# A gap in a modulation schedule, three pinned readers and later row transposes in a macaron layer

## The chip, the cores and the metric

The kernel runs on one core of one Trainium2 chip. The metric is the device time of one execution in microseconds (us); before the change the median of three runs is 1946.7 us (1944.29 to 1949.12). Everything below about times of the kernel before comes from one more, profiled execution.

## The reference, cut to what matters

One decoder layer for 256 tokens of width 2048, all in float32. A vector `c` gives nine modulation vectors of 2048 values each; three blocks (FFN, mixer, FFN) use a shift, a scale and a gate each.

```python
mod = silu(c) @ ada_w + ada_b                      # 9 * 2048 values
sh1, sc1, gt1, sh2, sc2, gt2, sh3, sc3, gt3 = split(mod, 9)
h = rmsnorm(x, g0) * (1 + sc1) + sh1
x = x + 0.5 * gt1 * (silu(h @ wg0) * (h @ wu0)) @ wd0      # FFN 1, inner width 5632
h = rmsnorm(x, g1) * (1 + sc2) + sh2
q_f, k_f, v_f, f_f, qkv_g, a_g, b_g, z_g = split(h @ w_in)
o_f = rmsnorm(forgetting_attention(q_f, k_f, v_f, log_sigmoid(f_f + bias)))   # 8 heads of 128
q_g, k_g, v_g = split(silu(causal_conv4(qkv_g)))
o_g = gated_delta_rule(l2norm(q_g), l2norm(k_g), v_g, decay(a_g), sigmoid(b_g))  # chunks of 64
o_g = rmsnorm(o_g) * silu(z_g)                             # 8 heads of 128
x = x + gt2 * (concat(o_f, o_g) @ w_out)
h = rmsnorm(x, g2) * (1 + sc3) + sh3
x = x + 0.5 * gt3 * (silu(h @ wg1) * (h @ wu1)) @ wd1      # FFN 2
return rmsnorm(x)
```

## The kernel before, in words

**Weight blocks.** All weight matrices are packed into one list of 128x128 tiles in the order of use, eight tiles (512 KB) to a block, 674 blocks. For every block SP issues a DMA into `wraw` (line 125), ACT casts it to the rounded form `whi` (line 128), and DVE subtracts to get the rest, `wlo` (line 140); PE multiplies with both, which gives float32 accuracy. There are four buffers each of `wraw`, `whi` and `wlo`; in the two FFNs every fifth block uses a further buffer for `wraw`. The stages by block number: FFN 1 gate and up for the first 28 of 44 column groups 0 to 112, its down product 112 to 168, gate and up for the rest 168 to 232, down 232 to 264; mixer projections 264 to 378, output projection 378 to 410; FFN 2 410 to 674.

**Modulation columns.** The modulation is computed beside this stream, 128 values at a time: one *column* is a DMA of 1 MB into `adat` (line 261) and one DVE reduction of it against silu(c) (line 265). There are 144 columns in the order of first need. `RATE` is a list of (block, columns per block); at every block the rate is added to `owed` (line 143), and whenever that reaches one, the next column is asked for. A column that is needed and hasn't been asked for is asked for at once (`ada_need`, line 274). The DMA is kept behind the DMA of the newest weight block; the reduction is recorded when the stream is two blocks further (`settle`, `BEHIND = 2`), behind the split of that block.

**Order of work.** A scheduler orders the recorded instructions of each engine by their estimated times; `issue_after(X)` keeps an instruction behind X in that order. In the mixer, small pieces of work (generators) are woven into the projections: each `yield g` lets g us of estimated matmul time (0.35 us per tile of three matmuls) pass before the generator goes on. There are four queues of them: `k`, `gdn`, `fox` and `out`. Queue `k` holds in order `gates` (line 829), then `decays(0)`, `keys(0)` to `keys(3)`, `solve(0)`, and `decays(1)`, `keys(4)` to `keys(7)`, `solve(1)`.

**Small DRAM round trips.** Three kinds of data go through DRAM to be spread over the partitions. `gates` transposes the gate projections (`pcol`, line 844), computes log decays, makes rows and columns of their cumulated sums (`prow`, `pcum`, lines 877 to 886) and stores the rows; `row_of` (line 903) and `fetch_rows` (line 927) read them back into `rw` and `rowk` by SP. Readers of these are `decay(h)`, which adds a mask to `rw` into `dec` (line 914) and takes exponentials on ACT (lines 916, 917); `decays(half)`, which subtracts `rowk` from a mask into `Ln` for four heads (line 935) and takes eight exponentials (line 938); and `fox(h)`, whose mask `fm` starts as two ACT operations on `rw` (line 1184), followed by logits, a maximum (line 1195), exponentials (line 1199), and a transpose `ppt` of them on PE (line 1204). `solve` stores blocks of `Ln` (eight DMAs, line 999), reads them back, solves 16x16 systems on DVE (lines 1012, 1013), stores (line 1018) and reads the result `U` (line 1022), from which two DVE operations make `U0` (line 1025). `keys(h)` transposes a key (`pk`, line 971), makes its Gram matrix (`pkk`, line 974), takes norms (line 977) and a copy (line 978) on ACT and multiplies the Gram matrix into `Ln` (line 984).

Of the kernel before, what the change touches and what calls it, by code (L numbers as in the profile page):

```python
# [12 lines left out]
AF = mybir.ActivationFunctionType  # L13
ALU = mybir.AluOpType
PSUM = bass.MemoryType.PSUM

P = 128
# [15 lines left out]
GR = 24  # L33
NEG = -1e30

RATE = ((0, 0.5), (28, 0.25), (33, 0.5), (49, 0.25), (56, 0.5), (66, 0.2), (112, 0.5), (168, 0.42), (232, 0.24), (264, 0.0), (288, 0.285), (376, 0.0), (424, 0.16))
N_BIG, N_GDN = 3, 3
N_FIRST = 2
AHEAD = 4
# [54 lines left out]
class Stream:  # L94
# [36 lines left out]
    def next(self, mat, k, n, width=1):  # L131
        i = len(self.order)
        if i % WB == 0:
            nc = self.nc
            b = i // WB
            r, lo = self.first.pop(0) if self.first else self.block(b)
            self.l = lo.tile([P, WB * P], F32R, name="wlo")
            pace = [r_ for r_ in RATE if r_[0] <= b][-1][1]
            with self.behind():
                lo_ = nc.vector.tensor_tensor(self.l, r, self.h.bitcast(F32), ALU.subtract)  # L140
            with self.tc.issue_after(lo_.ins):
                self.settle(b - BEHIND)
            self.owed += 0.0 if self.quiet else pace
            while self.owed >= 1.0:
                self.owed -= 1.0
                self.side()
        for d in range(width):
            self.order.append((mat, k, n, width, d))
        o = (i % WB) * P
        h, l = self.h[:, o : o + width * P], self.l[:, o : o + width * P]  # L150
        return (h, l) if width == 1 else (woven(h), woven(l))
# [3 lines left out]
def layer_kernel(ctx: ExitStack, tc: tile.TileContext, xrow, c, adaw, cols, cst, w, out, order, dbg=None):  # L155
    nc = tc.nc
    V, A, G, PE = nc.vector, nc.scalar, nc.gpsimd, nc.tensor
# [26 lines left out]
    W = Stream(nc, w, raw, hi, lo)  # L184
# [40 lines left out]
    def C(name, lo_=0, n=None):  # L225
        o, wd = CST[name]
        return cstt[:, o + lo_ : o + (wd if n is None else lo_ + n)]
# [449 lines left out]
    for kind, i in (("x", 0), ("x", 1), ("c", 0), ("c", 1), ("x", 2), ("x", 3), ("c", 2), ("c", 3)):  # L677
        with nullcontext() if hold is None else tc.issue_after(hold):
            if kind == "c":
                hold = cond(i)  # L680
            else:
                t, q = divmod(i, 2)
# [70 lines left out]
    def mixer():  # L753
# [65 lines left out]
        colS = gp.tile([P, 2, 5, NH], F32, name="colS")  # L819
# [7 lines left out]
        Ln = gp.tile([P, NH, 2, P], F32, name="Ln")  # L827
        U0 = gp.tile([P, NH, 2, 64], F32, name="U0")

        def gates(ps):  # L830

            yr = x[:, 8]
            d = pt("ey")
            s = norm1.scaled(d, ps)
            A.activation(yr[R], d[R], AF.Identity, bias=s[R])
            y, ny, e, em, t0, q = (x[:, j, : 2 * GR].rearrange("p (t r) -> p t r", t=2) for j in range(10, KD))
            coef = tiny.tile([P, GR + PAD["hid"]], F32, name="coef", bufs=1)[:, :GR]
            tc.keep_in_program_order(A.activation(coef, L("alog"), AF.Exp))
            V.tensor_scalar(coef, coef, -1.0, None, ALU.mult)
            yield 2.0  # L840
            pc = psf("pcol")
            pcv = pc[:, : 2 * GR].rearrange("p (t r) -> p t r", t=2)
            for t in range(2):
                PE.transpose(pcv[:, t], yr[R, t * P : (t + 1) * P], ident[R, :GR])
            both = lambda c_: c_.unsqueeze(1).to_broadcast([P, 2, GR])
            V.tensor_tensor(y, pcv, both(L("gbias")), ALU.add)
            V.tensor_tensor(y, y, both(C("sgn")), ALU.mult)
            V.scalar_tensor_tensor(ny, y, -1.0, y, ALU.mult, ALU.min)
            A.activation(e, ny, AF.Exp)
            V.tensor_scalar(em, y, 0.0, None, ALU.min)  # L850
            A.activation(em, em, AF.Exp)

            S = ny
            V.tensor_scalar(t0, e, 2.0, None, ALU.add)
            V.reciprocal(t0, t0)
            V.tensor_tensor(S, e, t0, ALU.mult)
            V.tensor_tensor(t0, S, S, ALU.mult)
            V.tensor_scalar(q, t0, 1.0 / 17.0, None, ALU.mult)
            for n in (15, 13, 11, 9, 7, 5, 3):
                V.scalar_tensor_tensor(q, q, 1.0 / n, t0, ALU.add, ALU.mult)  # L860
            V.scalar_tensor_tensor(q, q, 1.0, S, ALU.add, ALU.mult)
            V.tensor_scalar(y, y, 0.0, None, ALU.max)
            V.scalar_tensor_tensor(y, q, 2.0, y, ALU.mult, ALU.add)
            V.tensor_tensor(y, y, both(coef), ALU.mult)

            V.tensor_scalar(t0, e, 1.0, None, ALU.add)
            V.reciprocal(t0, t0)
            V.tensor_tensor(colS[:, :, 4], em[:, :, 16:24], t0[:, :, 16:24], ALU.mult)
            yield 8.0

            fox_, gdn_ = slice(0, NH), slice(NH, 2 * NH)
            pr = psf("prow")
            po = psf("pcum")
            pcs = po[:, : 6 * NH].rearrange("p (t q r) -> p t q r", t=2, q=3)
            for t in range(2):
                sl = slice(t * P, (t + 1) * P)
                PE.matmul(pr[:NH, T + t * P : T + (t + 1) * P], y[:, t, gdn_], C("tri64"), start=True, stop=True)
                PE.matmul(pr[:NH, sl], y[:, t, fox_], C("tri"), start=True, stop=(t == 0))
                if t:
                    PE.matmul(pr[:NH, sl], y[:, 0, fox_], L("ones"), start=False, stop=True)  # L880
            for t in range(2):
                PE.matmul(pcs[:, t, 1], C("tri64"), y[:, t, gdn_], start=True, stop=True)
                PE.matmul(pcs[:, t, 2], C("tru64"), y[:, t, gdn_], start=True, stop=True)
                PE.matmul(pcs[:, t, 0], C("tri"), y[:, t, fox_], start=True, stop=(t == 0))
                if t:
                    PE.matmul(pcs[:, t, 0], L("ones"), y[:, 0, fox_], start=False, stop=True)
            rt = x[:, 8:10].rearrange("p a t -> p (a t)")[:NH]
            A.copy(rt, pr[:NH])
            nc.sync.dma_start(rows, rt)
            V.tensor_copy(colS[:, :, 0:2], pcs[:, :, 0:2])  # L890
            A.activation(colS[:, :, 2:4], pcs[:, :, 1:3], AF.Exp)
            V.tensor_tensor(nbeg, colS[:, :, 4], colS[:, :, 2], ALU.mult)
            V.tensor_scalar(nbt, colS[:, :, 4], -1.0, None, ALU.mult)
            V.tensor_scalar(ng, colS[:, :, 1], -1.0, None, ALU.mult)
            yield 2.0
            fetch_rows(0)
            yield 1.0
# [8 lines left out]
        bc = lambda c_: c_.unsqueeze(1).to_broadcast([P, 2, P])  # L906
        bh = lambda c_, n: c_.unsqueeze(1).to_broadcast([n, 2, 64])

        def decay(h):

            gb = rowg.pop(h)
            gbv = gb.rearrange("p (t j) -> p t j", t=2)
            dd = m2p.tile([P, 2, P], F32, name="dec")
            V.tensor_tensor(dd, bc(C("mU")), gbv, ALU.add)
            for t in range(2):
                A.activation(dd[:, t], dd[:, t], AF.Exp, bias=ng[:, t, h : h + 1])
            A.activation(gb, gb, AF.Exp)
            return dd, gb
# [10 lines left out]
        def decays(half):  # L929

            hs4 = slice(4 * half, 4 * half + 4)
            yield 5.0
            rv = rowk[half].rearrange("p h (t j) -> p (h t) j", t=2)
            mL = C("mL").unsqueeze(1).to_broadcast([P, 8, P])
            V.tensor_tensor(Ln[:, hs4].rearrange("p h t j -> p (h t) j"), mL, rv, ALU.subtract)
            for h in range(4 * half, 4 * half + 4):
                for t in range(2):
                    A.activation(Ln[:, h, t], Ln[:, h, t], AF.Exp, bias=colS[:, t, 1, h : h + 1])
            yield 3.0
# [46 lines left out]
        def solve(half):  # L986


            hs4, n = slice(4 * half, 4 * half + 4), 2 * NH // 2
# [14 lines left out]
            blk, xt_, pr = (x[B, j] for j in range(4, 7))  # L1004
# [15 lines left out]
            U = x[:, 7, :P].rearrange("p (n i) -> p n i", n=n)  # L1020
# [1 line left out]
                nc.sync.dma_start(U, lt[ht].rearrange("n b (q i) -> (b q) n i", q=16))  # L1022
            yield 5.0
            for q in range(2):
                V.tensor_tensor(
                    U0[:, hs4].rearrange("p h t (b i) -> p (h t) b i", b=4)[:, 4 * q : 4 * q + 4],
                    U[:, 4 * q : 4 * q + 4].unsqueeze(2).to_broadcast([P, 4, 4, 16]),
                    C("blk").unsqueeze(1).unsqueeze(3).to_broadcast([P, 4, 4, 16]), ALU.mult)
            if half == 0:
                fetch_rows(1)  # L1030
            yield 1.0
# [148 lines left out]
        def fox(h, qk, vt):  # L1180
            cb = rowf.pop(h)
            fm = m1p.tile([P, 384], F32, name="fm")
            for t, o, wd in ((0, 0, P), (1, P, T)):
                A.activation(fm[:, o : o + wd], cb[:, :wd], AF.Identity, bias=colS[:, t, 0, h : h + 1], scale=-1.0)
            V.tensor_tensor(fm, fm, C("foxm"), ALU.add)
            yield 1.5
            pl = psf("plog")
# [293 lines left out]
```

## Time and profile before

| | |
|---|---|
| median of three runs | 1946.7 us |
| the profiled execution | 1951.09 us |
| its span, first to last instruction | 1949.1 us |
| mean granted TensorE clock | 0.992 |
| blocks 0 to 112 of FFN 1 on PE | about 19 to 341 us |
| blocks 112 to 168, 168 to 232, 232 to 264 | to 494, 665, 749.5 us |
| mixer projections from block 264 | from 749.5 us |

The profiled execution took 1951.09 us, 4.4 us more than the median, and 2 us of it lie outside of the span. Lines of the profile name the engine, the source line, what is written from what, the shape, the count, the busy time and the mean of one instruction, then the idle time ahead of it and what ended most of that. The views of waits give, for a stretch of time, who waited for whom: us in total, how many times, the longest. The views of windows give, for a stretch, the busy time of PE, of its weight loads (PEld), of DVE, ACT and POOL, then the granted clock of PE, the share of the time that the 16 DMA engines were busy, and the GB/s moved.

### The profile page before, as it was taken

What the parts mean: (1) busy time and instruction counts of PE and PEld (TensorE: products, weight loads), DVE (VectorE), ACT (ScalarE), POOL (GpSimd) and SP (SyncE); (2) the same over time, 40 slices, a digit from 0 to 9 for tenths busy, and PEclk for the clock granted to TensorE, in tenths of its full rate; (3) what the DMA queues carried; (4) which work ended last, traced back from release to release, by engine and by line L of the source; (5) the groups of instructions that cost most, each with busy time, mean ns of one, the idle gap of its engine ahead of it and who ended that gap; (6) DMA issues with size and microseconds to landing.
All of it is one profiled execution on the core that took longest, in us unless ns stands there. A gap on an engine that the chain in (4) does not pass through costs nothing.

```text
span 1949.1 us, 33807 instructions
## 1 busy us (share of the span) xinstructions
PE 1906.4 (98%) x13086; PEld 1777.7 (91%) x13087; DVE 1569.0 (81%) x2455; ACT 1051.7 (54%) x1670; POOL 52.3 (3%) x55
## 2 busy tenths in 40 slices
PE   9999999999999999999999999999999999999998
PEld 7999999888889999889989999999999999999997
DVE  6999978999999999779988978887777756566654
ACT  7444544433454557848666756665554345555553
POOL 0000000000000021000000002100000000000011
PEclk9999999999999999999999999999999999999999
DMA  9988877999999886486667647677787666666663
GB/s 383 347 347 330 319 249 268 388 378 385 362 358 368 333 280 226 170 295 235 236 239 274 218 138 252 206 269 263 267 267 264 224 199 203 202 200 202 201 202 119
DMA packets 129490, 519.58 MB, mean 267 GB/s; under 512 B 18217, under 2 KB 21545, under 8 KB 111153
## 3 DMA queue, kind: packets, MB, share of 16 engines
q1 hardware_dynamic: 129330, 517.42, 74.5%
q8 instruction: 103, 1.69, 0.3%
q14 instruction: 57, 0.47, 0.1%
HBM read 512.89 MB, written 4.47 MB: 265 GB/s over the span
## 4 chain that ended last, share of the span: by engine, by line
PE 73%; DVE 13%; issue 5%; DMA 5%; ACT 2%; SPq 0%; DVEq 0%; ACTq 0%
PE pd L488 14%; PE pu L484 10%; PE pg L484 10%; PE pd L489 7%; PE pu L485 5%; PE pg L485 5%; DVE wlo L140 5%; PE po L488 3%; DVE adat L265 3%; DMA adat<-in_ada_dram 3%; PE pgu L570 2%; PE pgu L568 2%; PE pgu L569 2%; PE pp L799 2%; PE pp L797 2%
## 5 line engine op out<-in xcount | busy, mean ns | idle before, releaser
L140 DVE TENSOR_TENSOR wlo<-wraw,whi 128x1024 fp32r<-128x1024 f32 x674 | 819.6, 1222 | 255.8 <-ACT whi L128 253.4
L128 ACT CAST whi<-wraw 128x1024 fp32r<-128x1024 f32 x674 | 698.2, 1045 | 501.2 <-PE pd L488 152.7
L488 PE MATMUL pd<-hid,whi 128*128 128x512 f32 x1408 | 461.8, 382 | 0.0
L489 PE MATMUL pd<-hid,wlo 128*128 128x256 f32 x1408 | 384.5, 273 | 4.3 <-DVE wlo L140 4.3
L265 DVE CUSTOM_DVE_ANT_0 adat<-adat,cs,colt 128x2048 f32<-128x2048 f32 x142 | 333.0, 2345 | 18.1 <-DMA adat<-in_ada_dram 18.1
L484 PE MATMUL pg<-hs,whi 128*128 128x512 f32 x912 | 302.5, 382 | 0.5 <-DVE shc L432 0.5
L484 PE MATMUL pu<-hs,whi 128*128 128x512 f32 x912 | 302.3, 382 | 0.0
L488 PEld LDWEIGHTS pd<-hid,whi 128*128 128x128 f32 x1408 | 266.0, 189 | 36.6
L489 PEld LDWEIGHTS pd<-hid,wlo 128*128 128x128 f32 x1408 | 270.3, 192 | 7.2 <-DVE wlo L140 7.0
L570 PE MATMUL pgu<-hs,wlo 128*128 128x256 f32 x896 | 240.8, 279 | 13.6 <-DVE wlo L140 13.1
L485 PE MATMUL pu<-hs,wlo 128*128 128x256 f32 x912 | 249.3, 273 | 0.4 <-DVE wlo L140 0.2
L485 PE MATMUL pg<-hs,wlo 128*128 128x256 f32 x912 | 249.5, 274 | 0.0
L568 PE MATMUL pgu<-hs,whi 128*128 128x256 f32 x896 | 244.7, 276 | 0.4 <-ACT whi L128 0.3
L569 PE MATMUL pgu<-hs,whi 128*128 128x256 f32 x896 | 244.2, 276 | 0.0
L484 PEld LDWEIGHTS pg<-hs,whi 128*128 128x128 f32 x912 | 172.4, 189 | 24.7 <-ACT shc L431 0.7
L484 PEld LDWEIGHTS pu<-hs,whi 128*128 128x128 f32 x912 | 172.4, 189 | 23.6
L570 PEld LDWEIGHTS pgu<-hs,wlo 128*128 128x128 f32 x896 | 168.6, 193 | 17.5 <-DVE wlo L140 17.4
L485 PEld LDWEIGHTS pu<-hs,wlo 128*128 128x128 f32 x912 | 175.0, 192 | 2.5 <-DVE wlo L140 2.4
L485 PEld LDWEIGHTS pg<-hs,wlo 128*128 128x128 f32 x912 | 175.0, 192 | 1.1
L568 PEld LDWEIGHTS pgu<-hs,whi 128*128 128x128 f32 x896 | 172.6, 193 | 1.1 <-ACT whi L128 0.5
L797 PE MATMUL pp<-hs,whi 128*128 128x256 f32 x592 | 172.5, 291 | 0.4 <-ACT whi L128 0.4
L569 PEld LDWEIGHTS pgu<-hs,whi 128*128 128x128 f32 x896 | 172.6, 193 | 0.3 <-DVE hs L382 0.3
(346 smaller groups left out, 2653.7 us busy)
## 6 DMA issues: line engine op xcount, KB each, us to landing
wraw<-in_w_dram SPq DMA_DIRECT2D x674, 512.0 KB, 4.5
adat<-in_ada_dram SPq DMA_DIRECT2D x142, 1024.0 KB, 7.4
xr<-in_xr_dram SPq DMA_DIRECT2D x4, 512.0 KB, 5.4
adaf<-in_ada_dram SPq DMA_DIRECT2D x4, 512.0 KB, 8.6
xd<-x SPq DMA_DIRECT2D x4, 512.0 KB, 6.7
rw<-rowd SPq DMA_DIRECT2D x16, 128.0 KB, 6.2
x<-xd SPq DMA_DIRECT2D x4, 512.0 KB, 7.1
out_dram<-o SPq DMA_DIRECT2D x8, 256.0 KB, 2.8
```

Of the source, the lines that this page charges most:

```text
L128: self.cast = self.nc.scalar.copy(self.h, r).ins
L140: lo_ = nc.vector.tensor_tensor(self.l, r, self.h.bitcast(F32), ALU.subtract)
L265: V.tensor_tensor_reduce(t, t, cs, 1.0, L("adab", q, 1), ALU.mult, ALU.add, mod[:, q : q + 1])
L484: PE.matmul(ps, wt[0], both, start=(k == 0), stop=False)
L485: PE.matmul(ps[:, T:], wt[1], part(k, HI), start=False, stop=(k == KD - 1))
L488: PE.matmul(ps, wt[0], act.rearrange("p q (a b) -> p q b a", a=2), start=first, stop=False)
L489: PE.matmul(ps[:, :T], wt[1], woven(act[:, 0]), start=False, stop=last)
L568: PE.matmul(o, wh, part(k, HI), start=first and s == 0, stop=False, skip_group_check=skip)
L569: PE.matmul(o, wh, part(k, LO), start=False, stop=False, skip_group_check=skip)
L570: PE.matmul(o, wl, part(k, HI), start=False, stop=last, skip_group_check=skip)
L797: PE.matmul(pp[i][:, :T], wh, hh, start=(k == 0), stop=False)
L799: PE.matmul(pp[i][:, :T], wl, hh, start=False, stop=(k == KD - 1))
```

## The change

Four edits, none of which changes what is computed. (1) `RATE` gets an entry of zero from block 90, so that no column is asked for in blocks 90 to 111; the later rates go from 0.42 to 0.45 (168 to 231), 0.24 to 0.26 (232 to 263) and 0.285 to 0.295 (from 288), and the last of these ends at block 384 and not 376. (2) `gates` waits 4 us of estimated time and not 2 before its transposes `pcol`. (3) `decays(1)` starts after 10 us and not 5. (4) The readers of the small DRAM transfers are kept behind a split or a cast: the first operations of `decay` and `decays` and the `U0` operations of `solve` behind the newest split (`W.split`, which `Stream.next` now keeps), the two `fm` operations of `fox` behind the newest cast.

```diff
@@ -33,7 +33,7 @@
 GR = 24
 NEG = -1e30
 
-RATE = ((0, 0.5), (28, 0.25), (33, 0.5), (49, 0.25), (56, 0.5), (66, 0.2), (112, 0.5), (168, 0.42), (232, 0.24), (264, 0.0), (288, 0.285), (376, 0.0), (424, 0.16))
+RATE = ((0, 0.5), (28, 0.25), (33, 0.5), (49, 0.25), (56, 0.5), (66, 0.2), (90, 0.0), (112, 0.5), (168, 0.45), (232, 0.26), (264, 0.0), (288, 0.295), (384, 0.0), (424, 0.16))
 N_BIG, N_GDN = 3, 3
 N_FIRST = 2
 AHEAD = 4
@@ -140,6 +140,7 @@
                 lo_ = nc.vector.tensor_tensor(self.l, r, self.h.bitcast(F32), ALU.subtract)
             with self.tc.issue_after(lo_.ins):
                 self.settle(b - BEHIND)
+            self.split = lo_.ins
             self.owed += 0.0 if self.quiet else pace
             while self.owed >= 1.0:
                 self.owed -= 1.0
@@ -837,7 +838,7 @@
             coef = tiny.tile([P, GR + PAD["hid"]], F32, name="coef", bufs=1)[:, :GR]
             tc.keep_in_program_order(A.activation(coef, L("alog"), AF.Exp))
             V.tensor_scalar(coef, coef, -1.0, None, ALU.mult)
-            yield 2.0
+            yield 4.0
             pc = psf("pcol")
             pcv = pc[:, : 2 * GR].rearrange("p (t r) -> p t r", t=2)
             for t in range(2):
@@ -911,7 +912,8 @@
             gb = rowg.pop(h)
             gbv = gb.rearrange("p (t j) -> p t j", t=2)
             dd = m2p.tile([P, 2, P], F32, name="dec")
-            V.tensor_tensor(dd, bc(C("mU")), gbv, ALU.add)
+            with tc.issue_after(W.split):
+                V.tensor_tensor(dd, bc(C("mU")), gbv, ALU.add)
             for t in range(2):
                 A.activation(dd[:, t], dd[:, t], AF.Exp, bias=ng[:, t, h : h + 1])
             A.activation(gb, gb, AF.Exp)
@@ -929,10 +931,11 @@
         def decays(half):
 
             hs4 = slice(4 * half, 4 * half + 4)
-            yield 5.0
+            yield 10.0 if half else 5.0
             rv = rowk[half].rearrange("p h (t j) -> p (h t) j", t=2)
             mL = C("mL").unsqueeze(1).to_broadcast([P, 8, P])
-            V.tensor_tensor(Ln[:, hs4].rearrange("p h t j -> p (h t) j"), mL, rv, ALU.subtract)
+            with tc.issue_after(W.split):
+                V.tensor_tensor(Ln[:, hs4].rearrange("p h t j -> p (h t) j"), mL, rv, ALU.subtract)
             for h in range(4 * half, 4 * half + 4):
                 for t in range(2):
                     A.activation(Ln[:, h, t], Ln[:, h, t], AF.Exp, bias=colS[:, t, 1, h : h + 1])
@@ -1022,10 +1025,11 @@
                 nc.sync.dma_start(U, lt[ht].rearrange("n b (q i) -> (b q) n i", q=16))
             yield 5.0
             for q in range(2):
-                V.tensor_tensor(
-                    U0[:, hs4].rearrange("p h t (b i) -> p (h t) b i", b=4)[:, 4 * q : 4 * q + 4],
-                    U[:, 4 * q : 4 * q + 4].unsqueeze(2).to_broadcast([P, 4, 4, 16]),
-                    C("blk").unsqueeze(1).unsqueeze(3).to_broadcast([P, 4, 4, 16]), ALU.mult)
+                with tc.issue_after(W.split):
+                    V.tensor_tensor(
+                        U0[:, hs4].rearrange("p h t (b i) -> p (h t) b i", b=4)[:, 4 * q : 4 * q + 4],
+                        U[:, 4 * q : 4 * q + 4].unsqueeze(2).to_broadcast([P, 4, 4, 16]),
+                        C("blk").unsqueeze(1).unsqueeze(3).to_broadcast([P, 4, 4, 16]), ALU.mult)
             if half == 0:
                 fetch_rows(1)
             yield 1.0
@@ -1181,7 +1185,8 @@
             cb = rowf.pop(h)
             fm = m1p.tile([P, 384], F32, name="fm")
             for t, o, wd in ((0, 0, P), (1, P, T)):
-                A.activation(fm[:, o : o + wd], cb[:, :wd], AF.Identity, bias=colS[:, t, 0, h : h + 1], scale=-1.0)
+                with tc.issue_after(W.cast):
+                    A.activation(fm[:, o : o + wd], cb[:, :wd], AF.Identity, bias=colS[:, t, 0, h : h + 1], scale=-1.0)
             V.tensor_tensor(fm, fm, C("foxm"), ALU.add)
             yield 1.5
             pl = psf("plog")
```

From here on each reduction and split is counted by its block. In the order of the changed kernel columns 36 to 41 are asked for behind the DMAs of blocks 112, 114, 116, 118, 120 and 122, where it was 90, 95, 100, 105, 110 and 113 (counted from 0; each later column of FFN 1 comes 6 to 10 blocks later than before, columns 100 and 101 come at 289 and 292 instead of 252 and 256, the rest 7 to 4 later in the mixer and 2 earlier in FFN 2). Column 127, which was forced by its use at block 410, is now asked for by rate at 380. By stretches, 6 columns were asked for in blocks 90 to 113 and now one; in 114 to 167 it is 27 in both; in 168 to 231 it is 27 before and 29 now, in 232 to 263 it is 6 and 7, and in 288 to 383 it is 25 and 28. All lines from 143 on have moved by one to five.

On DVE, behind the split of block 87, before (line 265 is a reduction, lines 586, 587, 519 and 503 are the ends of gate and up products):

```order
L140 TENSOR_TENSOR wlo<-wraw,whi 128x1024
L265 ISA adat,mod<-adat,cs,colt 128x2048
L265 ISA mod 128x1
L586 TENSOR_TENSOR tg<-pgu,acc 128x256
L587 TENSOR_TENSOR tu<-pgu,acc 128x256
L140 TENSOR_TENSOR wlo<-wraw,whi 128x1024
L519 TENSOR_TENSOR tu<-tu,tg 128x256
L140 TENSOR_TENSOR wlo<-wraw,whi 128x1024
L503 TENSOR_TENSOR hid<-tu,hid 128x256
```

and in the changed kernel, from the splits of blocks 87 and 88:

```order
L140 TENSOR_TENSOR wlo<-wraw,whi 128x1024 x2
L587 TENSOR_TENSOR tg<-pgu,acc 128x256
L588 TENSOR_TENSOR tu<-pgu,acc 128x256
L520 TENSOR_TENSOR tu<-tu,tg 128x256
L140 TENSOR_TENSOR wlo<-wraw,whi 128x1024
L504 TENSOR_TENSOR hid<-tu,hid 128x256
```

The reduction between two splits is gone; the same holds behind the splits of blocks 92, 97, 102, 107 and 111. The first reduction of the changed kernel after that of column 35 stands behind the split of block 109, four element operations later.

On ACT in the mixer, from the casts of blocks 283 and 284 on, before (`j` and `kk` are of `keys(0)`, `fm` of `fox(0)`, `kbd` of the first `gdn`, `Ln` of `decays(0)`; ACT_TABLE_LOAD loads another function table):

```order
L128 CAST whi<-wraw 128x1024 x2
L977 ACTIVATE j_9118,ssk<-pk 128x128
L977 ACTIVATE j_9120,ssk<-pk 128x128
L978 COPY kk<-pk 128x256
L1184 ACTIVATE fm<-rw,colS 128x128
L1184 ACTIVATE fm<-rw,colS 128x256
L1084 ACTIVATE kbd<-kk,colS 128x128
L938 ACT_TABLE_LOAD
L938 ACTIVATE Ln<-Ln,colS 128x128 x8
L959 ACT_TABLE_LOAD
```

and in the changed kernel, from the cast of block 283 on, with the cast of block 284 in the fifth row:

```order
L128 CAST whi<-wraw 128x1024
L962 ACT_TABLE_LOAD
L962 ACTIVATE kk<-cv 128x256
L959 ACTIVATE cv<-cp,colt 128x256
L128 CAST whi<-wraw 128x1024
L941 ACT_TABLE_LOAD
L941 ACTIVATE Ln<-Ln,colS 128x128 x8
L962 ACT_TABLE_LOAD
L962 ACTIVATE kk<-cv 128x256
L955 COPY cp<-pp 128x256
```

The norms of `keys(0)`, `fm` and `kbd` stand no longer between the cast and the exponentials. Between the exponentials and the next cast, of block 285, stand ten rows (a table load, `kk`, `cp`, `cv`, four `j`, two copies of `kk`), where it was seven with two `j` and one copy. `fm` now stands behind the cast of block 302.

On ACT some blocks later, behind the casts of blocks 302 and 303, before (`x<-x,fmx` are the exponentials of `fox(0)`, `Ln` of `decays(1)`):

```order
L128 CAST whi<-wraw 128x1024 x2
L1278 ACTIVATE x<-pp 128x256
L938 ACT_TABLE_LOAD
L938 ACTIVATE Ln<-Ln,colS 128x128 x6
L1199 ACTIVATE x,fzz<-x,fmx 128x128
L1199 ACTIVATE x,fzz<-x,fmx 128x256
L938 ACTIVATE Ln<-Ln,colS 128x128 x2
L128 CAST whi<-wraw 128x1024 x2
```

and in the changed kernel, behind the casts of blocks 304 to 306:

```order
L128 CAST whi<-wraw 128x1024 x3
L955 COPY cp<-pp 128x256
L1204 ACT_TABLE_LOAD
L1204 ACTIVATE x,fzz<-x,fmx 128x128
L1204 ACTIVATE x,fzz<-x,fmx 128x256
L959 ACTIVATE cv<-cp,colt 128x256
L918 ACTIVATE dec<-dec,ng 128x128
L1211 COPY x<-ppt 128x384
L918 ACTIVATE dec<-dec,ng 128x128
L919 ACTIVATE rw<-rw 128x256
L941 ACTIVATE Ln<-Ln,colS 128x128
L962 ACT_TABLE_LOAD
```

The exponentials of `decays(1)` have moved from ahead of the cast of block 304 to behind that of 306, where those of `fox(0)` now stand too. Before the cast of block 307 follow ten rows more: two `qv`, two `j`, one `cp`, two table loads, seven `Ln` in two rows and one `cv`. On DVE the `Ln` operation of line 935 stood behind the split of block 303 and now stands behind that of 306; the `U0` operations stay behind the split of 302. On PE the transposes `pcol` and the matmuls `prow` and `pcum` stand at the same places as before, between the same tiles of blocks 275 and 278. On SP the stores of `Ln` blocks now follow the DMA of block 291, the store of line 1018 comes before a read of `rw`, and the read of line 927 for the second half follows the DMA of block 304 and not that of 303.

## The prediction

> **What bounds the kernel now.** I read the page first. Its first line of busy times says that PE is the bound over the span as a whole.
>
> ```profile
> PE 1906.4 (98%) x13086; PEld 1777.7 (91%) x13087; DVE 1569.0 (81%) x2455; ACT 1051.7 (54%) x1670; POOL 52.3 (3%) x55
> L140 DVE TENSOR_TENSOR wlo<-wraw,whi 128x1024 fp32r<-128x1024 f32 x674 | 819.6, 1222 | 255.8 <-ACT whi L128 253.4
> L265 DVE CUSTOM_DVE_ANT_0 adat<-adat,cs,colt 128x2048 f32<-128x2048 f32 x142 | 333.0, 2345 | 18.1 <-DMA adat<-in_ada_dram 18.1
> adat<-in_ada_dram SPq DMA_DIRECT2D x142, 1024.0 KB, 7.4
> ```
>
> PE is busy for 1906.4 of 1949.1 us, so nothing in this change, which takes no matmul away, can save more than the 43 us in which PE stands still plus what a lower clock costs. What can be won lies in the few stretches with gaps. I looked for these with the view of windows, stretch by stretch.
>
> ```profile
> 257.00:345.00 88.00, 80.47 (x703) 79.12 (x703) 71.01 (x112) 43.03 (x66) 0.00 (x0) 1.00 0.71 252
> 276.00:293.00 17.00, 15.23 (x136) 15.04 (x136) 12.00 (x17) 8.10 (x11) 0.00 (x0) 1.00 0.71 241
> 342.00:420.00 78.00, 76.44 (x465) 70.13 (x466) 74.69 (x91) 33.50 (x36) 0.00 (x0) 1.00 0.97 389
> 499.00:603.00 104.00, 103.64 (x625) 93.74 (x624) 96.35 (x111) 52.57 (x79) 0.00 (x0) 1.00 0.97 364
> 603.00:661.00 58.00, 57.93 (x351) 52.47 (x350) 55.00 (x64) 29.15 (x44) 0.00 (x0) 1.00 0.93 351
> 780.00:800.00 20.00, 18.36 (x147) 17.65 (x146) 15.65 (x47) 18.29 (x29) 0.00 (x0) 0.91 0.41 133
> 812.00:834.00 22.00, 19.63 (x90) 16.77 (x89) 12.25 (x35) 16.08 (x38) 0.00 (x0) 0.92 0.44 154
> 868.00:894.00 26.00, 21.33 (x156) 20.18 (x155) 18.45 (x46) 17.93 (x44) 0.43 (x2) 0.87 0.86 305
> ```
>
> After the stretch's bounds and length stand the busy times of PE, PEld, DVE, ACT and POOL, the granted clock, the DMA share and GB/s. PE lacks 7.53 us in 257 to 345 (blocks 85 to 113), almost nothing from 499 to 661, and 1.64, 2.37 and 4.67 us in three short stretches of the mixer, where the clock is also down: 0.09 x 20 = 1.8, 0.08 x 22 = 1.8 and 0.13 x 26 = 3.4 us. These four places are the ones that the change touches.
>
> **Columns out of blocks 90 to 111.** The waits of 257 to 345 say whose fault the 7.53 us are, and the timeline of DVE shows one case.
>
> ```profile
> DVE adat L265 <- DMA adat<-in_ada_dram: 13.4, 5, 3.5
> PE pgu L570 <- DVE wlo L140: 6.0, 5, 1.8
> PE pd L489 <- DVE wlo L140: 1.5, 1, 1.5
> ...
> 276.90 1.23 DVE L140 TENSOR_TENSOR wlo<-wraw,whi 128x1024 fp32r<-128x1024 f32 x1 [0.52 <-ACT whi L128]
> 281.59 2.35 DVE L265 CUSTOM_DVE_ANT_0 adat<-adat,cs,colt 128x2048 f32<-128x2048 f32 x1 [3.46 <-DMA adat<-in_ada_dram]
> 284.54 1.21 DVE L140 TENSOR_TENSOR wlo<-wraw,whi 128x1024 fp32r<-128x1024 f32 x1
> ```
>
> The reduction stands ahead of the next split and comes to its turn before its column has landed (7.4 us after issue at the median). DVE waits 3.46 us, reduces for 2.35, and the split that PE needs starts 7.64 us after the one before, where PE uses up a block in some 2.6 us. Six waits of PE, 6.0 + 1.5 = 7.5 us, are all of the idle time there. In the changed order none of the reductions behind the splits of 87 to 107 is left. The new first one, behind the split of block 109, finds PE with its full lead of four `wlo` buffers and may cost up to one such wait (at most 1.8), but the rhythm of splits behind each wait is saved too, which the idle time alone doesn't count. I take **-7.5**, bounds -6 and -9.
>
> **Blocks 112 to 167** keep 27 columns, later by 9 or 10 blocks; the waits of 345 to 500 price what can move.
>
> ```profile
> DVE x L512 <- PE pd L489: 8.6, 8, 2.4
> PE pd L489 <- DVE wlo L140: 2.3, 7, 0.6
> ```
>
> DVE waits eight times for the end of a product, with a split behind it, and PE pays 2.3 us in seven waits. In the changed order the first columns come later, and I count one or two fewer places where a reduction stands between such a product and the next split: 1.5 x 0.33 = **-0.5**, bounds -1.5 and +1.
>
> **Blocks 168 to 263** get three columns more. DVE is busy 96.35 of 104 us there and the DMA engines 0.97 of the time; the timeline shows the tightest case.
>
> ```profile
> 541.28 0.42 DVE L503 TENSOR_TENSOR hid<-tu,hid 128x256 fp32r<-128x256 f32 x1
> 541.62 2.34 DVE L265 CUSTOM_DVE_ANT_0 adat<-adat,cs,colt 128x2048 f32<-128x2048 f32 x1
> 543.89 0.42 DVE L496 TENSOR_TENSOR tg<-pg,mg 128x256 f32<-128x256 f32 x1
> 544.22 1.21 DVE L140 TENSOR_TENSOR wlo<-wraw,whi 128x1024 fp32r<-128x1024 f32 x1
> PEld pu L485 <- DVE wlo L140: 2.4, 7, 0.5
> ```
>
> Such a row of four works without an idle gap and costs at most 0.5 us (the last line, waits of 500 to 745); seven cost 2.4. DVE's own work hides the rest, since a block gives DVE 2.66 us (104 us for 625/16 = 39 blocks) and each split takes 1.22. Three more columns are 7.0 us of DVE against 7.65 idle in 104 us alone, so they fit. I take **+0.6** for two further rows, bounds 0 and +3. Without that cover each would cost its 2.35.
>
> **`pcol` 4 us and not 2 later.** The wait is PE's for ACT, 1.6 us, plus the 1.8 of clock.
>
> ```profile
> PE pcol L844 <- ACT x L835: 1.6, 1, 1.6
> ```
>
> In the order `pcol`, `prow` and `pcum` have not moved by one matmul against the tiles around them, so the wait stays. The clock after it may not: the stretch from 276 has as much idle time (1.77 us) and a clock of 1.00. I take **-0.5**, bounds -1.7 and +0.5. The Trainium skill, page "TensorE: Matmul & The Clock Gate", section "What's actually happening", says that PE goes to half clock after an idle window of about 3.4 us, which is free-running; by that rule neither the wait of 1.6 nor one of 2.4 would lower the clock, and what is saved at the next place would be the idle time alone, some 1.5 us less. The rows at 0.91 and 0.92 speak against that rule here, and the measurement decides.
>
> **The first `decays`.** In 812 to 834 PE lacks 2.37 us and 1.8 of clock, 4.1 together. The waits of 800 to 834 and ACT's timeline:
>
> ```profile
> PE pkk L974 <- ACT kk L978: 2.4, 1, 2.4
> ...
> 803.14 1.98 ACT L128 CAST whi<-wraw 128x1024 fp32r<-128x1024 f32 x2
> ...
> 808.31 0.80 ACT L1184 ACTIVATE fm<-rw,colS 128x128 f32<-128x128 f32 x2 [2.08 <-DMA rw<-rowd]
> 809.02 0.39 ACT L1084 ACTIVATE kbd<-kk,colS 128x128 f32<-128x128 f32 x1
> ...
> 810.72 2.45 ACT L938 ACTIVATE Ln<-Ln,colS 128x128 f32<-128x128 f32 x8
> ...
> 816.21 1.07 ACT L128 CAST whi<-wraw 128x1024 fp32r<-128x1024 f32 x1
> ```
>
> PE waits for the copy of `pk`, which stands in ACT's row behind `fm`, and `fm` waits 2.08 us for `rw`. From the end of one cast (805.12) to the next (816.21) it is 11.1 us. In the changed order `fm` (0.80 and its 2.08) and `kbd` (0.39) are gone from there, and a `kk` norm pair is added (two of 0.28 and a copy of 0.38): 11.1 - 3.3 + 0.9 = 8.7 at most, less where the first norms move too. The hole shrinks by 2.4 to 3.4, and PE's idle time of 2.4 goes for the most part, with part of the clock. I take **-2.8**, bounds -4 (all) and +1. What is late next is the row of exponentials itself, 2.45 and two table loads.
>
> **The second `decays` and `fox(0)`.** In 868 to 894 the loss is 4.67 + 3.4 = 8.1.
>
> ```profile
> ACT Ln L938 <- DVE Ln L935: 4.8, 1, 4.8
> PE ppt L1204 <- ACT x L1199: 2.7, 1, 2.7
> 872.58 1.86 ACT L938 ACTIVATE Ln<-Ln,colS 128x128 f32<-128x128 f32 x6 [4.77 <-DVE Ln L935]
> 877.22 1.98 ACT L128 CAST whi<-wraw 128x1024 fp32r<-128x1024 f32 x2
> ```
>
> ACT stands 4.77 us in front of exponentials whose mask DVE cannot make before `rowk` has landed; the cast of block 304 is queued behind them. The change moves the exponentials behind the cast of block 306, past three casts, and with them the read of `rowk` on SP's queue behind the DMA of block 304. By then the wait has gone, but the same ACT row now holds both sets of exponentials and four table loads before the cast of block 307. At the durations of the same forms (eight exponentials 2.45, a group of four operations of `fox(0)` 1.3, four table loads of 1.28, `kk` copies and casts of `cp` 0.4 each) this row is about 14 us. Three casts ahead of it give PE 3 x 2.6 = 7.8 us, so PE lacks about 6.2 and some clock, 7.1 in all: **-1**. Bounds: -5 where PE's small matmuls and a fourth buffer cover most of the row, +5 where the `wlo` splits are held too and the clock falls for longer.
>
> **The rest of the mixer** gets three columns more in 288 to 383, 7 us of DVE, of which 18.45 of 26 us are busy at the worst place: **+0.5**, bounds 0 and +2. The pinned readers that don't wait now cost nothing: they stay in their rows, hidden by DVE's idle time there.
>
> **The sum**: -7.5 - 0.5 + 0.6 - 0.5 - 2.8 - 1 + 0.5 = -11.2 us. Against the profiled 1951.09 that is 1939.9; the median of the runs stands 4.4 lower, so I forecast 1946.7 - 11.2 = **1935.5**.
>
> **Rivals.** *The columns cost as much later.* The five that leave blocks 90 to 111 land where DVE and the DMA engines are fuller, at 1.5 us each (7.5 / 5) they take the first term back, and the time is 1943. For it speaks the DMA share of 0.97 in 499 to 603; against it that there, with 0.42 columns a block, PE loses only 0.36 of 104 us. *Only the columns pay*: the long ACT row stalls PE by 5 and the first `decays` saves nothing; -11.2 + 2.8 + 1 + 2 = -5.4, 1941 at most, 1939 in the middle. *Slower: landings outrun the lead.* Between 500 and 603 a column is asked for and reduced like this (DMA issues, then SP and DVE):
>
> ```profile
> adat<-in_ada_dram SPq DMA_DIRECT2D x16, 1024.0 KB, 8.2
> 527.65 0.46 SPq L261 DMA_DIRECT2D adat<-in_ada_dram  x1
> ```
>
> It lands 8.2 us after issue at the median, and by the order of columns it is the one reduced at 541.62, 14 us after: a slack of 5.8. If the higher rate fills the DMA engines (0.97 now) so that landings pass 14 us, DVE waits in front of splits as it did in 276 to 285. That decides from there; at 1.5 us for every second of the 36 columns of blocks 168 to 263 it is +27, at a third +18, and I price it at 1953. *DMA bound.* The Trainium skill, page "DMA: Bandwidth & Descriptors", section "Where 436 GB/s comes from", lets the HBM side bind at about 358 GB/s a core. A block of 0.524 MB and 0.45 columns of 1.049 MB in 2.66 us are 374 GB/s; if a bound lay at the 364 of 499 to 603, a block would take 2.74 and 64 blocks 5 us more, 1940.5. By the page's figure it would be an estimated 2.78 and 8 us more. The 389 GB/s of 342 to 420 speak against either. *The change doesn't do what it says* holds for one edit only, `pcol`, and is in the sum.
>
> **Chances.** Forecast 0.60, only columns 0.16, columns dear later 0.12, slower 0.09, DMA bound 0.03. Under 1940.9 or over 1952.5 is what a measurement of this kernel can tell from no change (0.3%). Faster: 0.59 + 0.12 + 0.02 = 0.73; same: 0.01 + 0.03 + 0.07 + 0.01 = 0.12; slower: 0.01 + 0.03 + 0.09 + 0.02 = 0.15. The range: the bounds of the terms, not all at their ends, give -22 to the low side, 1925, and 1923 with the spread of runs; on the high side 1946 takes in the first two rivals and leaves 0.15 out.
>
> **What would show it.** Waits of PE for `wlo` in 257 to 345 near nothing, PE busy over 86 of 88 us; at 168 to 232 waits under 3 us and no wait of DVE for `adat`; no `fm` in front of the first exponentials and a clock of 0.95 or more there; a long row without a cast on ACT ahead of block 307. Wrong it would be by new waits of DVE for `adat` past block 112, or by a gap at block 307 of 10 us or more.

## The result and the profile after

The changed kernel takes 1944.43 us (median of 17 runs, 1942.93 to 1947.11), the kernel before 1948.84 in as many runs beside it (1942.38 to 1953.88): 4.4 us less, a ratio of 0.9978 with an interval of 0.9968 to 0.9988. The forecast was 11.2 us less. The profiled executions stand 6.5 us apart, 1944.62 against 1951.09.

Page of the changed kernel:

```profile
PE 1902.1 (98%) x13086; PEld 1774.6 (91%) x13087; DVE 1570.4 (81%) x2455; ACT 1047.1 (54%) x1668; POOL 53.5 (3%) x55
L266 DVE CUSTOM_DVE_ANT_0 adat<-adat,cs,colt 128x2048 f32<-128x2048 f32 x142 | 332.9, 2344 | 7.3 <-DMA adat<-in_ada_dram 7.3
```

The counts of PE, PEld and DVE instructions are those of before, and DVE's idle time in front of reductions fell from 18.1 to 7.3 us. To see where the time went I took PE's first matmul of each block from both traces; the table gives PE's time between blocks, before and as a difference.

| blocks | before, us | changed, difference | forecast |
|---|---|---|---|
| 85 to 113 | 84.1 | -9.1 | -7.5 |
| 113 to 168 | 148.3 | -0.5 | -0.5 |
| 168 to 232, 232 to 264 | 170.8, 84.6 | **+6.3**, -0.8 | +0.6 for both |
| 264 to 278 (`pcol`) | 43.1 | -1.6 | -0.5 |
| 278 to 290 (first `decays`) | 41.4 | -3.6 | -2.8 |
| 290 to 302 | 32.0 | +0.1 | |
| 302 to 308 (second `decays`) | 27.9 | **+1.9** | -1 |
| 308 to 378, 378 to 673 | 259.4, 780.7 | +1.1, -0.1 | +0.5 |

The differences sum to -6.2. At the bounds 290 and 308 matmuls of two tiles interleave in some kernels; the expectations below set these bounds 0.2 to 0.3 us differently. Three places of the forecast, blocks 85 to 113, `pcol` and the first `decays`, are there and a little larger. Windows of the changed kernel (bounds, length, PE, PEld, DVE, ACT, POOL, clock, DMA share, GB/s), in the order of the table:

```profile
257.00:345.00 88.00, 88.00 (x759) 87.13 (x759) 71.65 (x115) 47.55 (x72) 0.00 (x0) 1.00 0.72 245
484.00:662.00 178.00, 172.25 (x1032) 155.11 (x1031) 163.93 (x190) 84.36 (x127) 0.00 (x0) 1.00 0.95 358
801.00:825.00 24.00, 24.00 (x126) 21.17 (x125) 18.83 (x47) 18.05 (x47) 0.00 (x0) 1.00 0.63 235
856.00:887.00 31.00, 24.54 (x184) 23.32 (x183) 21.55 (x45) 22.14 (x45) 0.42 (x2) 0.89 0.65 253
```

PE had 80.47 of 88 us in 257 to 345 and has all 88; the gap at the first `decays` is closed too. In the first of these stretches the weight loads had waited for splits, before, like this (us in total, times, longest):

```profile
PEld pgu L570 <- DVE wlo L140: 6.9, 5, 2.0
PEld pd L489 <- DVE wlo L140: 1.8, 1, 1.8
```

But in blocks 168 to 232, where before PE lacked 0.36 of 104 us and 0.07 of 58, it now lacks 5.75 of 178, and at block 302 to 308 it loses 6.46 us and a clock of 0.89. The waits of PE for splits in blocks 168 to 232 of the changed kernel:

```profile
PEld pu L486 <- DVE wlo L140: 8.4, 9, 2.3
PE pu L486 <- DVE wlo L140: 5.5, 3, 2.0
```

Nine waits are 8.4 us where seven were 2.4, and three of them make 6.4 us: one each at blocks 182, 202 and 222, 20 blocks apart. DVE's timeline at the first of them:

```profile
517.72 1.23 DVE L140 TENSOR_TENSOR wlo<-wraw,whi 128x1024 fp32r<-128x1024 f32 x1 [0.52 <-ACT whi L128]
518.86 0.42 DVE L520 TENSOR_TENSOR tu<-tu,tg 128x256 f32<-128x256 f32 x1
519.77 0.43 DVE L504 TENSOR_TENSOR hid<-tu,hid 128x256 fp32r<-128x256 f32 x1 [0.49 <-ACT hid L503]
520.11 2.35 DVE L266 CUSTOM_DVE_ANT_0 adat<-adat,cs,colt 128x2048 f32<-128x2048 f32 x1
522.38 1.22 DVE L140 TENSOR_TENSOR wlo<-wraw,whi 128x1024 fp32r<-128x1024 f32 x1
```

No DMA is waited for. The reduction stands behind `hid`, which waits for ACT, and right ahead of the split of block 182. That split starts at 522.38; its cast on ACT was ready at 520.68, as the timeline of ACT shows:

```profile
519.31 0.43 ACT L503 CAST hid<-tu 128x256 fp32r<-128x256 f32 x1 [1.63 <-DVE tu L520]
519.64 1.04 ACT L128 CAST whi<-wraw 128x1024 fp32r<-128x1024 f32 x1
```

In the order these are three rows of `hid`, reduction, split; the kernel before has none of them. Six more have `tg` between the reduction and the split and cost 0.33 each. On ACT at block 306, the other loss (timeline, first and last of the row):

```profile
863.64 1.05 ACT L128 CAST whi<-wraw 128x1024 fp32r<-128x1024 f32 x1 [2.73 <-DMA wraw<-in_w_dram]
866.70 1.05 ACT L128 CAST whi<-wraw 128x1024 fp32r<-128x1024 f32 x1 [2.01 <-DMA wraw<-in_w_dram]
867.65 0.36 ACT L955 COPY cp<-pp 128x256 f32<-128x256 f32 x1
868.03 1.28 ACT L1204 ACT_TABLE_LOAD   x1
...
876.85 1.85 ACT L941 ACTIVATE Ln<-Ln,colS 128x128 f32<-128x128 f32 x6
878.71 1.28 ACT L962 ACT_TABLE_LOAD   x1
880.01 0.42 ACT L962 ACTIVATE qv<-cv 128x256 f32<-128x256 f32 x1
880.33 1.98 ACT L128 CAST whi<-wraw 128x1024 fp32r<-128x1024 f32 x2
```

Between two casts lie 12.6 us (867.75 to 880.33), and the casts ahead of this row had themselves waited 2 to 3 us for their weights. The two long waits of PE in 856 to 887 are for operations that stand in this row:

```profile
PE pvq L1056 <- ACT qv L962: 2.9, 1, 2.9
PE ppt L1209 <- ACT x L1204: 2.3, 2, 2.2
```

`x` is the exponential of `fox(0)` behind the first table load, and `qv` is the last operation ahead of the next cast, behind the exponentials `Ln`. PE comes to block 307, whose cast starts at 880.33, only at 882.10, so no idle time of PE is put down to that cast here.

### The profile page after: what moved, and what is told of

The parts are those of the page before. It is cut to its first block, busy times and chain, and to the rows that moved or that the text cites. A ratio compares the mean times of both kernels' runs of the same rounds, so it can differ in the third digit from the quotient of the medians.

```text
span 1942.8 us, 33800 instructions
## 1 busy us (share of the span) xinstructions
PE 1902.1 (98%) x13086; PEld 1774.6 (91%) x13087; DVE 1570.4 (81%) x2455; ACT 1047.1 (54%) x1668; POOL 53.5 (3%) x55
## 5 line engine op out<-in xcount | busy, mean ns | idle before, releaser
L489 PEld LDWEIGHTS pd<-hid,whi 128*128 128x128 f32 x1408 | 266.3, 189 | 36.8
L485 PEld LDWEIGHTS pu<-hs,whi 128*128 128x128 f32 x912 | 172.6, 189 | 23.4
L798 PE MATMUL pp<-hs,whi 128*128 128x256 f32 x592 | 170.8, 289 | 0.2 <-ACT whi L128 0.2
```

The lines of the kernel that those rows point to most:

```text
L485: PE.matmul(ps, wt[0], both, start=(k == 0), stop=False)
L489: PE.matmul(ps, wt[0], act.rearrange("p q (a b) -> p q b a", a=2), start=first, stop=False)
L798: PE.matmul(pp[i][:, :T], wh, hh, start=(k == 0), stop=False)
```

## The experiments

**The two halves of the change apart.** First the new `RATE` alone:

```diff
 before, with
-RATE = (..., (66, 0.2), (112, 0.5), (168, 0.42), (232, 0.24), (264, 0.0), (288, 0.285), (376, 0.0), (424, 0.16))
+RATE = (..., (66, 0.2), (90, 0.0), (112, 0.5), (168, 0.45), (232, 0.26), (264, 0.0), (288, 0.295), (384, 0.0), (424, 0.16))
```

> The new schedule of columns alone, all edits of the mixer undone. If the loss of the changed kernel in blocks 168 to 231 (PE 177.1 us there against 170.8 before) comes from the schedule, it stands here too: blocks 88 to 113 gain 9.1, 114 to 167 gain 0.5, 168 to 231 lose 6.3, 232 to 263 gain 0.8, and the mixer is as before within 1.5, in all 4 us less than before. The rival, that the mixer's edits carry the gain and the schedule is worth nothing, gives the time of before within 1.

Measured: 1939.16 us, a ratio to before of 0.9944 (0.9932 to 0.9956). Up to block 264 it is the changed kernel to 0.1 us, the +6.3 included, so the schedule alone makes that loss; its waits there are word for word the same amounts:

```profile
PEld pu L485 <- DVE wlo L140: 8.4, 9, 2.3
PE pu L485 <- DVE wlo L140: 5.5, 3, 2.0
```

But the mixer is not as before: blocks 302 to 308 take 6.2 us less, and 264 to 378 together 7.5 less, with none of the mixer's edits. That the parts are separate was wrong. Then the mixer's edits with the old `RATE`:

```diff
 after, with
-RATE = (..., (90, 0.0), (112, 0.5), (168, 0.45), (232, 0.26), (264, 0.0), (288, 0.295), (384, 0.0), ...)
+RATE = (..., (112, 0.5), (168, 0.42), (232, 0.24), (264, 0.0), (288, 0.285), (376, 0.0), ...)
```

> The old schedule with the edits of the mixer. By the theory that the parts are separate: no gain before block 264 (the six waits for wlo of 7.5 us come back), 170.8 us in blocks 168 to 231, then -1.6 at pcol's clock, -3.4 at the first decays and +2 at the second, about 3 us less than before. The rival, that the long ACT row at block 306 comes from the edits to the mixer, shows a gap of 5 or more there; if it comes from the later columns, the stretch of blocks 302 to 308 takes no longer than before.

Measured: 1949.6 us, ratio 0.9994 (0.9984 to 1.0005), no change that can be told; the 3 us expected lie at the edge of the interval. The stages of the profiled execution: +0.5 in 85 to 113, -4.3 at the first `decays`, +2.1 in blocks 302 to 308, -1.6 in 308 to 378, and nothing at `pcol`. So the long ACT row comes with the edits of the mixer under the old schedule as under the changed one, while the new schedule without them has the gain there.

**Place or load in blocks 168 to 231.** The old rates there and in 232 to 263:

```diff
 after, with
-(168, 0.45), (232, 0.26)
+(168, 0.42), (232, 0.24)
```

> The changed kernel with the old rates 0.42 and 0.24 in blocks 168 to 263. Both theories of the loss there, the place of the reductions and the load, expect 171 to 173 us in blocks 168 to 231 (177.1 in the changed kernel): five reductions between hid and tg at 0.33 each and none between hid and a split. In all 4 to 6 us less than the changed kernel, if the mixer stays the same.

Measured: 1935.51 us, ratio 0.9922 (0.9909 to 0.9934), 8.9 us under the changed kernel. 170.4 us in blocks 168 to 231. In the mixer blocks 302 to 308 gained 4.9 where the changed kernel lost 1.9, so it did not stay the same; 308 to 378 gave 5.0 back. Both theories allow this; the next two do not.

```diff
 after, with
-(112, 0.5), (168, 0.45)
+(112, 0.5), (167, 0.60), (168, 0.45)
```

> The changed kernel with 0.60 instead of 0.50 columns in block 167 alone, so that the same 0.45 of blocks 168 to 231 runs one tenth of a column ahead. By the theory of place (three reductions that stand between hid and the next split cost 2.1 each) these three rows are gone from the order and eight of 0.33 are left: 172 to 173.5 us in blocks 168 to 231. By the theory of load (0.45 is more than DVE and the DMA engines hold) nothing changes there: 176 to 178 us.

Measured: 1935.13 us, ratio 0.9922 (0.9909 to 0.9935). A tenth of a column in one block takes 3.6 of the 6.3 us back: 173.5 us, at the upper end of what the theory of place had expected, at the same rate and with the same 29 columns. The waits for splits in 484 to 658 show one price more:

```profile
PEld pu L486 <- DVE wlo L140: 2.9, 11, 0.3
PEld pg L486 <- DVE wlo L140: 2.5, 3, 0.8
```

The three rows of `hid`, reduction, split are gone; at blocks 184, 204 and 224 a reduction stands alone between two splits in their place, at 0.8 each, which the expectation had not foreseen.

```diff
 after, with
-(168, 0.45)
+(168, 0.5)
```

> The changed kernel with 0.50 columns a block in blocks 168 to 231, 32 instead of 29, so that requests fall on even blocks only and the order holds fifteen rows of hid, reduction, tg, split and none of a reduction between hid and split. Theory of place: 15 x 0.33 = 5 us over the plain time of some 168.5, 173 to 175 us from block 168 to 232. Theory of load (DVE and the DMA engines filled by more columns): more than the 177.1 of the changed kernel, 179 to 185.

Measured: 1934.32 us in one run, and 173.8 us in blocks 168 to 231. Windows and waits of PE for splits in that stretch:

```profile
484.00:658.00 174.00, 173.48 (x1028) 154.27 (x1027) 169.12 (x196) 83.23 (x124) 0.00 (x0) 1.00 1.00 383
PEld pu L486 <- DVE wlo L140: 5.0, 15, 0.3
```

The stretch has 32 columns and takes less time than with the 29 of the changed kernel: fifteen rows of 0.33, 5.0 us, though DVE is busy for 169.12 of 174 us and the DMA engines all of the time. Load is not the cause. The price belongs to the place: 2.1 to 2.3 between `hid` and a split, 0.8 alone between two splits with the shifted phase, at most 0.34 between `hid` and `tg`, 0.13 ahead of `tu`, and nothing in the other places that recur.

**The gap alone.**

```diff
 before, with
-(66, 0.2), (112, 0.5)
+(66, 0.2), (90, 0.0), (112, 0.5)
```

> The kernel before with one edit: no columns in blocks 90 to 111, all later rates and the mixer as before. Theory: the gap is worth what the stretch shows (blocks 88 to 113 9.1 us, 114 to 167 0.5 us less) and nothing is given back in 168 to 231, where the order holds no reduction between hid and a split: 171 to 172 us there. Before block 264 it is 10 us less than before, and in all 1935 to 1940 us. The rival, that the columns left out come back as a loss in the mixer or by uses that force them there, gives 1944 or more.

Measured: 1939.61 us, ratio 0.9949 (0.9931 to 0.9968). -9.1, -0.5 and -0.3 in the three stretches, and 2.0 lost late, in blocks 410 to 420: five columns are asked for only in blocks 403 to 410, where they are first used. Blocks 264 to 378, where nothing was edited, took 5.3 us less too (6.5 in 302 to 308), so the whole is not the price of the gap's own stretch alone. One entry of the table gives more than twice what the whole change gave.

**The ACT row at block 306.** First without the pin of `dec`:

```diff
 after, in decay(h)
-            with tc.issue_after(W.split):
-                V.tensor_tensor(dd, bc(C("mU")), gbv, ALU.add)
+            V.tensor_tensor(dd, bc(C("mU")), gbv, ALU.add)
```

> The changed kernel without the pin on decay's first operation (dec is free to stand ahead of the split again). In the order the ACT row between the casts of blocks 306 and 307 loses dec, dec, rw and a qv and two Ln, about 3 us of some 12.6, since dec of the first head goes back to block 288. By the theory that this row is what PE waits for, the stretch from block 302 to 308 takes about 3 us less than in the changed kernel (36.8 there, 34.5 before), and the whole 2 to 4 us less. The rival, that late landings of weights (casts that wait 2 to 3 us for wraw at 858 to 867) set the loss there, gives 36 to 37.5 us.

The two absolute times in this expectation, 36.8 and 34.5, were misread; blocks 302 to 308 take 29.9 us in the changed kernel and 27.9 before. Measured: 27.9 us, 2.0 less and not 3, with a row of 10.9 us, and 1943.09 in all, ratio 0.9974 (0.9964 to 0.9985), not to be told from the changed kernel: 1.2 us are lost at block 293, where `dec` now stands. The wait for `qv` is gone, and PE now waits 1.0 and 0.5 us for the casts behind the row. This speaks for the row, but not clearly. The next one moves work and takes none away:

```diff
 after, in decays(half)
+            if half:
+                yield 6.0
             for h in range(4 * half, 4 * half + 4):
                 for t in range(2):
-                    A.activation(Ln[:, h, t], Ln[:, h, t], AF.Exp, bias=colS[:, t, 1, h : h + 1])
+                    with tc.issue_after(W.cast):
+                        A.activation(Ln[:, h, t], Ln[:, h, t], AF.Exp, bias=colS[:, t, 1, h : h + 1])
```

> The changed kernel, with the exponentials of the second decays 6 us of estimated time later and behind the newest cast. No work is added or left out; in the order the long ACT row between the casts of blocks 306 and 307 falls into three rows with casts between them (about 5, 3 and 4 us). Theory of the row: blocks 302 to 308 take 23 to 26 us and not 30.2 (27.9 before), and the whole is 4 to 7 us less than the changed kernel. The rival, that the amount of ACT work or the landing of weights sets it, gives 29 to 31 us.

Measured: 25.3 us in blocks 302 to 308, 4.6 less than in the changed kernel, of which 1.4 come back in 308 to 378, where some small matmuls of PE now stand; 1940.78 in all, ratio 0.9957 (0.9941 to 0.9974), 3.7 us under it. The pin behind the cast holds for `decays(0)` too, but 282 to 290 takes the same 23.4 us as in the changed kernel. ACT's timeline there has the same operations with casts between them, and the same late weights ahead:

```profile
866.84 1.05 ACT L128 CAST whi<-wraw 128x1024 fp32r<-128x1024 f32 x1 [1.88 <-DMA wraw<-in_w_dram]
...
871.91 0.41 ACT L919 ACTIVATE rw<-rw 128x256 f32<-128x256 f32 x1
872.22 1.03 ACT L128 CAST whi<-wraw 128x1024 fp32r<-128x1024 f32 x1
...
876.87 0.37 ACT L958 COPY cp<-pp 128x256 f32<-128x256 f32 x1
877.12 1.07 ACT L128 CAST whi<-wraw 128x1024 fp32r<-128x1024 f32 x1
...
879.90 2.45 ACT L944 ACTIVATE Ln<-Ln,colS 128x128 f32<-128x128 f32 x8
```

PE's waits of half a microsecond and more in 856 to 882 are these, and the one for `qv` is gone:

```profile
PE ppt L1212 <- ACT x L1207: 2.7, 1, 2.7
PE pp L800 <- DVE wlo L140: 0.8, 1, 0.8
```

So PE pays for what stands ahead of the operations that it needs in one undivided row, not for the amount of work. How much of it is `qv` behind the exponentials and how much the cast behind them, no run separates.

**The gates' transposes.**

```diff
 after, in gates
-            yield 4.0
+            yield 2.0
```

> The changed kernel with 2 us and not 4 ahead of pcol. By the prediction pcol stands at the same place either way, so the wait of 1.6 us stays, and the clock after it, 1.00 in the changed kernel and 0.91 before, is a matter of phase: PE's time from block 275 to 278 is 10.2 or 11.8. The rival: the later pcol row moves the key norms and thereby the ACT row at block 284, which then takes longer than in the changed kernel: blocks 282 to 290 at 22.5 to 24 us and not 23.2 (26.8 before).

Measured: 1944.71 us in one run, as the changed kernel, but by other stages. Blocks 264 to 278 are the same to 0.1 (the wait of `pcol` is 1.6 us in both), and 278 to 290 gain 1.8 instead of 3.6; the rival's stretch, 282 to 290, takes 22.9 us, no longer than the 23.4 of the changed kernel, and the 2.3 lost lie ahead of it, in 278 to 282, at half clock in part (0.50 from 793 to 795 us). In blocks 302 to 308 it gains 1.7 where the changed kernel loses 1.9, and in 308 to 378 it loses 3.5. The edit leaves `pcol` alone and shifts what follows.

**Together.** The shifted phase and a free `dec`:

```diff
 after, with
-(112, 0.5), (168, 0.45)
+(112, 0.5), (167, 0.60), (168, 0.45)
 and in decay(h)
-            with tc.issue_after(W.split):
-                V.tensor_tensor(dd, bc(C("mU")), gbv, ALU.add)
+            V.tensor_tensor(dd, bc(C("mU")), gbv, ALU.add)
```

> Both together: 0.60 columns in block 167, and dec free. 172 to 174 us in blocks 168 to 231, and in the mixer the ACT rows of over 4 us sum to 18 where the changed kernel has 29 in the order. 1931 to 1935 us, the fastest so far, if the row is the cause in the mixer; as the kernel with the shifted phase alone (1935) if it isn't.

Measured: 1932.47 us, ratio 0.9916 (0.9903 to 0.993), the fastest of all: 173.5 us in blocks 168 to 231, and 9.4 us less than before in 302 to 308, of which 1.2 come back in 308 to 378.

## Why the prediction was wrong

The sign and the mechanism of the first step held; the size of the whole was 2.5 times too large, because two terms went the other way.

- **Columns out of 90 to 111**, -7.5: -9.1, with PE busy in all of 257 to 345. The idle time of PE left something out, but not the rhythm of splits behind each wait, as the prediction had it: before, only blocks 88, 93, 98, 103, 108 and 112 take longer than the 2.68 us of the others there, by 9.1 in all, and the blocks behind them are back at 2.68. What PE's idle time leaves out is the weight load ahead of each waiting matmul, which waits longer: 8.7 us in all against 7.5. The first new reduction cost nothing that shows.
- **112 to 167**, -0.5: -0.5.
- **168 to 263**, +0.6 with a bound of +3: +6.3 - 0.8. **This is the step that failed.** It priced a row of `hid`, reduction, `tg`, split at 0.33 to 0.5, counted two more of these (five of the seven waits of before are such rows, and there is one more now), and reasoned that three more columns fit into DVE's idle time. They do fit; 32 of them did. But the order of the changed kernel also held three rows of `hid`, reduction, split, a form that the trace of before doesn't have, and that costs 2.1 to 2.3 each, 6.4 in all; the waits at 168 to 232, foreseen under 3 us, were 8.4. The reduction starts late because `hid` waits for ACT, and PE waits for the split behind it. The rival of columns that are dear later came to 1943, near the time measured, with five at 1.5; its reason, fuller engines, is refuted by the kernel at 0.50.
- **`pcol`**, -0.5: -1.6, all of it the clock, which was 1.00 in this execution; the wait of 1.6 us stayed. Nor does it belong to the edit: blocks 275 to 278 take 10.2 us in the runs of the schedule and of the gap without the edit, and 11.8 in two runs with it (the mixer's edits alone, and 0.50).
- **First `decays`**, -2.8: -3.6. The gap is closed; with the mixer's edits alone these blocks gain as much, 4.3.
- **Second `decays`**, -1, bounds -5 and +5: +1.9. The row was foreseen at 14 us and measured 12.6. PE's idle time, 6.46 us, came near the 6.2 foreseen, but by luck: it was to be one gap behind 7.8 us of lead from three casts, and it is waits for `x` and `qv` inside the row and one of 1.0 for the late cast and split of block 303. The clock was put at 0.9 and cost 0.11 x 31 = 3.4. Together that is 9.9 and not 7.1, against the 8.1 of before.
- **The rest of the mixer**, +0.5: +1.1 in 308 to 378 and +0.1 in 290 to 302.
- **DMA bound** and **landings that outrun the lead**: no wait of DVE for a column in blocks 168 to 232, and 383 GB/s at 0.50.

Of the 5.0 us between -11.2 and the -6.2 of the traces, the failed step makes 4.9 and the second `decays` 2.9, less 1.6, 1.1 and 0.8 at the three places that gained more; what is left, 0.7, lies in the rest of the mixer and in rounding. The medians, at -4.4, lie closer still; why executions of the kernel before scatter over 11.5 us and those of the changed kernel over 4.2 stays open.

Shown, by the kernel with the shifted phase and by one execution of the kernel with 0.50: the place and not the load in blocks 168 to 231. Shown by one kernel: that dividing the ACT row at block 306 takes time off. Not shown: why the same edits of the mixer give the long row under two schedules and shorter ones under others. The stages differ with it (302 to 308: +1.9 with 0.45, -4.9 with 0.42, -6.0 with 0.50), but over 302 to 378 it is +3.1, 0.0 and -4.8, so a short row does not pay by itself, and no run isolates the rule by which the scheduler makes the rows.

## What to carry to other kernels

Where a side task is spread over a pipeline by a rate, its period against the pipeline's own (20 blocks for nine columns here, four blocks for a group) decides where each piece falls, and a piece in the one bad place can cost its whole length: read the new order for forms of rows that the old one doesn't have, and don't price them by the forms that it has. An average load near full is no reason for a loss by itself. And a wait that is taken out of a strict row may gather the rest into one long row; count the time between two of the operations that feed the bottleneck, look for operations in the row that the bottleneck itself waits for, and check whether there is lead ahead of it.

## What the runs showed of the hardware

In the kernel with 0.50 columns a block the DMA engines moved 383 GB/s at a share of 1.00 for 174 us, and PE lost 0.52 us in that time. The Trainium skill, page "DMA: Bandwidth & Descriptors", section "Where 436 GB/s comes from", has about 358 GB/s bind on the HBM side for transfers from HBM; this kernel runs on one core, and the trace shows more. That is in line with the Trainium skill, page "DMA: Bandwidth & Descriptors", section "Measured (HBM→SBUF, 128 partitions, SWDGE, issued from GpSimd)", which has 425 GB/s for one core and the lower figure for two that share.

The granted clock differs at one place with the same waits ahead of it. Windows of three kernels with the same waits of PE just ahead and there (`pcol` 1.6 us, `prow` 0.6), the changed kernel, the one with 2 us ahead of `pcol`, and the one with the row split:

```profile
786.00:802.00 16.00, 15.40 (x134) 14.71 (x133) 14.32 (x36) 14.86 (x22) 0.00 (x0) 1.00 0.43 136
```

```profile
787.00:803.00 16.00, 15.40 (x123) 14.84 (x122) 12.69 (x31) 13.44 (x26) 0.00 (x0) 0.89 0.49 160
```

```profile
785.00:802.00 17.00, 16.40 (x129) 15.71 (x128) 13.86 (x34) 14.25 (x22) 0.00 (x0) 0.90 0.47 168
```

With equal gaps it is 1.00, 0.89 and 0.90, worth 1.6 to 2.3 us at this place (blocks 278 to 282). Before, it was lower some 10 us earlier: behind the one wait of 1.64 us for `pcol`, which ends at 784.5, it is 0.50 from 787 to 789 us, and the same wait in the changed kernel is followed by 1.00. A change should not be credited or blamed for such a term from one profile.
